# Moving large GpSimd operations to VectorE, and the first expert's input and weights in another order, ahead of a stream of 32 experts

## The chip, the cores and the metric

The kernel runs on one core of one Trainium2 chip. Inside the core five engines take their own instruction queues in parallel: TensorE (matrix products), VectorE, ScalarE and GpSimd (elementwise work), and SyncE, which here issues most of the DMA transfers. The metric is the device time of one execution in microseconds.

## The reference

One layer of a hybrid backbone is computed for 128 context rows and 256 latent rows of width 1024. The first half mixes an mLSTM head group and a Fourier head group behind one input projection and closes with a layer norm; the second half routes each row to 4 of 32 experts. Cut to what matters here:

```python
u = x * (1.0 + scale1) + shift1
p = u @ w_in                                   # q, k, v, o gate, gates, Fourier columns
h_m = layer_norm_per_head(mlstm(p)) * o_gate
f_m = fourier_mix(p[..., F_OFF:])              # Re of a 2-D DFT
mix = concatenate([h_m, f_m]) @ w_out
x = layer_norm(DEEPNORM_ALPHA * x + gate1 * mix, ln1_w, ln1_b)
u2 = x * (1.0 + scale2) + shift2
top_val, top_idx = lax.top_k(u2 @ router_w + router_b, TOP_K)
gates = softmax(top_val)
# for each expert e, on the rows that chose it:
h = xblk @ w_gu[e] + b_gu[e]
act = x_glu * sigmoid(SWIGLU_ALPHA * x_glu) * (x_lin + 1.0)
y += gate * (act @ w_down[e] + b_down[e])
x = layer_norm(DEEPNORM_ALPHA * x + gate2 * y, ln2_w, ln2_b)
```

All numbers are fp32, and the expert weights alone are 32 times 12 MB.

## The kernel before

The order is written out by hand: each engine runs its instructions in the order of the code, and waits there for whatever they need. So an instruction that waits holds up everything behind it on its engine.

**Phase 1, to about 180 us.** Modulation, input projection (`proj_T`, `proj_N`), mLSTM heads and Fourier groups. `proj_N(3, …)` computes the output gate (matmuls at L422); between its quarters it calls functions handed to it, in three gaps. Those that matter: `fourier_A` and `fourier_B` (VectorE L625 and L626, ScalarE L621 and L612), `head_norm` (VectorE L591), `mod_rest` (six small VectorE operations L668 to L673 on 64 partitions and less, which finish the modulation rows, and a DMA from ScalarE's queue, L674) and `wo_split`. The last cuts the output weights, eight pieces of 128x1024, into an upper part (ScalarE, L247) and the remainder (GpSimd, L249), since products of fp32 numbers are here summed from such parts. Pieces 0 to 3 belong to the first half of the output columns, 4 to 7 to the second. Then `ev_o` writes the gate: ScalarE's sigmoid (L491) and VectorE's product `og` (L492). TensorE transposes `og` (`heads_T`, L597), and L119, L120, L599 and L600 split the result.

**Phase 2, to about 241 us.** `out_mm` is the output projection (L853), `out_half` adds it to the residual (VectorE L860, L862, L864), `fold_1` and `fold_2` prepare the router's weights (VectorE L893 to L900, TensorE L904), `turn` transposes rows (TensorE L912, behind the L862 of the same rows), `router` gives the logits (L918), `top4` finds the four experts of each row (VectorE L923 to L946, for three groups of 128 rows: group 0 is the context, 1 and 2 the latent rows), and `places` counts (TensorE L950, behind L940 of `top4`). `out_norm(0)` normalises the context rows (ScalarE L883) and maps them to the expert's input with four GpSimd operations of 128x512 (L886, L887). `places_0` (VectorE L976, L977) and `gather_0` (TensorE L985) collect the rows of the first expert. How these follow each other is a string of steps (L1017): `m` is a part of the matmuls of rows 2, `h` of their `out_half`, `a` and `b` are single operations of the second and third `top4`, `A` and `B` their rest; letter and number are `P` places, `O` places_0, `T` turn, `R` router, `N` out_norm, `g` gather_0.

**Phase 3.** `experts` ends the order of the first stretch: the biases are split (L119, L120), and `modulate` maps the gathered rows to the first expert's input `XT0`, tiles 0 to 3 on ScalarE (L796), 4 to 7 on VectorE (L794), with an addition of 128x512 after each four (L797). Then 32 experts follow, each `gate_up` (L1163), activation, `down` (L1222), and spreading (L1107, L1241). Their weights are streamed by SyncE into a ring of tiles (`slot`, `fill`; the DMA issue is L755): a piece is issued when TensorE has finished with the piece whose tile it takes. The first expert's down projection is different (`load_dn`): piece 0 comes in two halves into the ring, piece 1 goes to tiles of its own (L781, L782).

## Time and profile before

| | |
|---|---|
| median of three runs | 1246.8 us (1244.35 to 1248.54) |
| profiled execution | 1248.78 us |
| its span, first to last instruction | 1247.1 us |
| mean granted clock of TensorE | 0.964 of full speed |
| TensorE busy | 1167.6 us (94%) |
| VectorE, ScalarE, GpSimd busy | 446.4, 229.0, 69.3 us |
| moved by DMA | 452.71 MB, mean 363 GB/s |

The span is read in three stretches: up to 180 us, where the work is varied; 180 to 244 us, where all engines work on the way to the first expert; and the experts, in which TensorE and the DMA engines are busy nearly all the time. A row of a timeline gives start, length, engine, line and tiles, and in brackets how long the engine stood idle before it and what ended that.

### The profile page before, as it was taken

To read this page: it belongs to the slowest core of one execution; us is meant where nothing else is said; L and a number is where in the kernel's file an instruction comes from. 1 tells how busy PE (TensorE), PEld (TensorE's weight loads), DVE (VectorE), ACT (ScalarE), POOL (GpSimd) and SP (SyncE) were. 2 spreads that over 40 slices of the span, in tenths; PEclk is the share of its full clock that TensorE was granted. 3 is DMA by queue.
4 is the path that set the end of the run, shared out by engine and by line. 5 is a ranking of instruction groups with operands and counts; after the bars stand their busy time and mean duration, and the time that the engine had idled before them with its cause. 6 is when DMAs were issued, how large, how long until landed. Compare 5 with 4: busy or idle time off the path is not lost.

```text
span 1247.1 us, 16409 instructions
## 1 busy us (share of the span) xinstructions
PE 1167.6 (94%) x6628; PEld 556.8 (45%) x6628; DVE 446.4 (36%) x944; ACT 229.0 (18%) x418; POOL 69.3 (6%) x79
## 2 busy tenths in 40 slices
PE   7999989799999999999999999999999999993874
PEld 4876768535335433434343353334435345331321
DVE  4444684623112431414323142332234124130415
ACT  2333341311211110201111121011111111111112
POOL 2001042200000000000000000000000000000301
PEclk9999989899899999999999999999999999996988
DMA  9977546499999999999999999999999899999993
GB/s 324 391 277 263 216 174 255 156 389 406 404 416 417 416 417 417 416 407 414 415 362 409 414 363 358 419 416 362 363 417 398 301 391 403 406 418 403 401 410 118
DMA packets 96978, 452.71 MB, mean 363 GB/s; under 512 B 8308, under 2 KB 18760, under 8 KB 62084
## 3 DMA queue, kind: packets, MB, share of 16 engines
q1 hardware_dynamic: 95088, 450.04, 91.0%
q10 hardware_dynamic: 1268, 1.31, 0.3%
q8 instruction: 54, 0.88, 0.3%
q0 software_dynamic: 544, 0.29, 0.1%
q14 instruction: 24, 0.20, 0.0%
HBM read 448.91 MB, written 2.70 MB: 362 GB/s over the span
## 4 chain that ended last, share of the span: by engine, by line
PE 84%; DMA 7%; DVE 5%; ACT 2%; issue 1%; SPq 1%; ACTq 0%; DVEq 0%
PE b L1163 38%; PE b L1222 19%; PE b L1241 4%; PE p L422 3%; DMA w<-in_w_gate_up_dram 3%; PE b L1107 3%; PE b L1171 2%; PE pm L853 2%; DMA w<-in_ln_w_dram 2%; PE b L1196 2%; DMA w<-in_w_ada_dram 1%; PE k L353 1%; ACT y L1228 1%; PE a L220 1%; DVE y L1230 1%
## 5 line engine op out<-in xcount | busy, mean ns | idle before, releaser
L1163 PE MATMUL b<-w,XT 128*64 128x512 f32 (+1 forms) x2560 | 496.2, 604 | 30.5 <-ACT w L1310 19.7
L1163 PEld LDWEIGHTS b<-w,XT 128*64 128x64 f32 (+1 forms) x2560 | 143.6, 129 | 332.2 <-issue 294.4
L1222 PE MATMUL b<-w,aT 128*64 128x512 f32 (+1 forms) x1596 | 248.3, 515 | 3.3 <-DMA w<-in_w_down_dram 3.2
L1182 DVE TENSOR_SCALAR g<-b 128x512 f32<-128x512 f32 (+1 forms) x40 | 24.5, 612 | 373.7 <-PE b L1171 293.9
L1222 PEld LDWEIGHTS b<-w,aT 128*64 128x64 f32 (+1 forms) x1596 | 81.6, 128 | 156.7 <-issue 141.9
L1230 DVE SCALAR_TENSOR_TENSOR y<-b,gc,y 64x512 fp32r<-64x512 f32 (+1 forms) x88 | 57.4, 652 | 217.6 <-ACT y L1228 217.3
L1228 ACT ACTIVATE y<-b,gc 64x512 fp32r<-64x512 f32 (+2 forms) x100 | 58.7, 587 | 292.1 <-PE b L1222 254.6
L1183 ACT ACTIVATE b<-g 128x512 f32<-128x512 f32 (+1 forms) x40 | 21.5, 538 | 353.6 <-DVE g L1182 353.4
L1246 DVE TENSOR_TENSOR yacc<-yacc,b 128x512 f32<-128x512 f32 x90 | 55.0, 680 | 0.0
L1107 PE MATMUL b<-O,tH 128*128 128x256 f32 x192 | 47.7, 289 | 4.5 <-DVE y L1230 4.5
L1241 PE MATMUL b<-y,OT 128*128 128x512 f32 x192 | 49.9, 405 | 0.0
L1317 POOL TENSOR_TENSOR XT<-tL,tH 128x384 f32<-128x384 f32 x2 | 2.0, 1006 | 841.5 <-PE b L1163 841.5
L1107 PE MATMUL b<-O,tL 128*128 128x256 f32 x192 | 46.5, 283 | 0.0
L1241 PEld LDWEIGHTS b<-y,OT 128*128 128x128 f32 x192 | 35.7, 193 | 13.9 <-issue 5.9
L1107 PEld LDWEIGHTS b<-O,tH 128*128 128x128 f32 x192 | 36.7, 191 | 10.2 <-DVE y L1230 5.3
L120 DVE TENSOR_TENSOR lw<-w,hw 128x1024 fp32r<-128x1024 f32 x20 | 24.4, 1222 | 34.9 <-ACT hw L119 34.7
L1107 PEld LDWEIGHTS b<-O,tL 128*128 128x128 f32 x192 | 36.7, 191 | 0.0
L1171 PEld LDWEIGHTS b<-bgu,pick 128*128 128x128 f32 x224 | 28.0, 189 | 18.7 <-issue 18.7
L1197 ACT ACTIVATE aT<-b 128x512 f32<-128x512 f32 (+1 forms) x40 | 21.3, 534 | 76.2 <-PE b L1196 70.9
L853 PE MATMUL pm<-w,mH 128*128 128x512 f32 x96 | 33.0, 426 | 0.0
L1171 PE MATMUL b<-bgu,pick 128*128 128x256 f32 x224 | 32.8, 292 | 0.0
L422 PE MATMUL p<-hw,uH 128*128 128x512 f32 x72 | 29.7, 412 | 1.7 <-ACT kq L412 1.7
(380 smaller groups left out, 1086.5 us busy)
## 6 DMA issues: line engine op xcount, KB each, us to landing
w<-in_w_gate_up_dram SPq DMA_DIRECT2D x113, 2048.0 KB, 13.4
w<-in_w_down_dram SPq DMA_DIRECT2D x52, 2048.0 KB, 15.5
w<-in_w_gate_up_dram SPq DMA_DIRECT2D x30, 1024.0 KB, 13.5
w<-in_w_down_dram SPq DMA_DIRECT2D x22, 1024.0 KB, 16.6
w<-in_w_ada_dram SPq DMA_DIRECT2D x8, 2048.0 KB, 7.6
w<-in_w_ada_dram SPq DMA_DIRECT2D x8, 1024.0 KB, 8.9
w<-in_w_in_dram SPq DMA_DIRECT2D x4, 2048.0 KB
w<-in_w_out_dram SPq DMA_DIRECT2D x2, 2048.0 KB, 8.8
```

The costliest lines, as they stand in the source:

```text
L422: PE.matmul(p[b], x, y, start=(k == 0 and t == 0), stop=(k == 7 and t == 2))
L853: PE.matmul(pm, x, y, start=(n == 0 and t == (part == 0) and part != 1), stop=(n == 7 and t == 2 and part != 0))
L1107: PE.matmul((pl if b else pc)[:, jj], t[b][:, (2 * i + jj) * 128:(2 * i + jj + 1) * 128], O[:, b], start=(b < 2 and q == 0), stop=(b != 1 ...
L1163: PE.matmul(p[g_][m * h:m * h + m], XT[:, k, o:o + m], rhs, start=(n_ == 0), stop=False, skip_group_check=True)
L1171: PE.matmul(p[g_][:, 256 * h:256 * h + 256], pick[2][:, h], bgu[:, q, 256 * g_:256 * g_ + 256], start=False, stop=(q == 1), skip_group_che ...
L1182: DVE.tensor_scalar(g, pg_, LIMIT, None, op0=OP.min)
L1196: PE.transpose(p[:, cc], s["act"][i][:, cc * 128:(cc + 1) * 128], ident)
L1222: PE.matmul(q[m * h:m * h + m, :f], aT[:, k, o:o + m], w[:, h * f:(h + 1) * f], start=(k == 0), stop=(k == 7))
L1228: ACT.activation(hi if plain else hi.bitcast(FR), dst, AF.Copy, scale=g)
L1230: DVE.scalar_tensor_tensor(y[1][o:o + m, h * f:(h + 1) * f].bitcast(FR), dst, g, hi, op0=OP.mult, op1=OP.subtract)
L1241: PE.matmul(p, OT[:, b * 128:(b + 1) * 128], y[q][:, hf * 512:(hf + 1) * 512].bitcast(FR), start=(u != 0 and q == 0), stop=(q == 1))
L1246: DVE.tensor_add(a, a, p)
```

## The change

There are four parts. The remainders of `wo_split` (L249) go from GpSimd to VectorE: those of pieces 2 and 3 into the second gap of `proj_N(3)`, piece 0 into the third, piece 1 behind `heads_T`, 4 to 7 where they stood in the code; in the second gap `mod_rest` now comes first. The context map goes from GpSimd to VectorE as two steps of the string, `X` behind `O0` and `Y` behind `g00`, and `g10` now stands between `P1` and `P2`. The first expert's input is mapped in the order in which TensorE uses its tiles, ahead of the bias split, with additions of 128x256. And of the first expert's down projection piece 1 is issued ahead of piece 0.

```diff
-            POOL.tensor_sub(l, w, h.bitcast(FT))
+            DVE.tensor_sub(l, w, h.bitcast(FT))
...
             wo_split(i, 0)
-            wo_split(i, 1)
-        proj_N(3, ev_o, lambda: (mod_loads(), fourier_B(0), fourier_A(2), head_norm(1), head_out(3), wo_split(2, 0), wo_split(2, 1), wo_split(3, 0), wo_split(3, 1)),
-               lambda: (fourier_B(1), fourier_A(3), mod_rest()),
-               lambda: (fourier_B(2), head_norm(2), head_norm(3), fourier_B(3)))
+        proj_N(3, ev_o, lambda: (mod_loads(), fourier_B(0), fourier_A(2), head_norm(1), head_out(3), wo_split(2, 0), wo_split(3, 0)),
+               lambda: (mod_rest(), fourier_B(1), fourier_A(3), wo_split(2, 1), wo_split(3, 1)),
+               lambda: (fourier_B(2), head_norm(2), head_norm(3), fourier_B(3), wo_split(0, 1)))
...
         heads_T()
+        wo_split(1, 1)
...
-        for i in range(2):
+        for i in (1, 0) if j == ORDER[0] else (0, 1):
...
-            for hs in halves:
-                POOL.tensor_mul(tX[b][:, hs], nc_[:, hs], bc["A", 1][:, hs])
-                POOL.tensor_add(tX[b][:, hs], tX[b][:, hs], bc["D", 1][:, hs])
+            context.append(nc_)
+
+        context = []
+
+        def context_map(hf):
+            hs = halves[hf]
+            DVE.tensor_mul(tX[0][:, hs], context[0][:, hs], bc["A", 1][:, hs])
+            DVE.tensor_add(tX[0][:, hs], tX[0][:, hs], bc["D", 1][:, hs])
...
-        for step in "P0 m m T1 m O0 R1 m g00 N1 h h T2 g01 a h a h a N2 a a a a R2 P1 b b b b b b b O1 P2 g11 A g10 O2 B C S g20 g21 E".split():
+        for step in "P0 m m T1 m O0 X R1 m g00 Y N1 h h T2 g01 a h a h a N2 a a a a R2 P1 b b b O1 b b b b g10 P2 A g11 O2 B C S g20 g21 E".split():
...
+        XT0 = mo.tile([128, 2, 8, 128], FT, name="XT", bufs=1)[:, 0]
+
+        for i, j in ((0, 2), (0, 3), (1, 4), (1, 5), (2, 2), (0, 0), (0, 1), (1, 6), (1, 7), (2, 0), (2, 4), (2, 6)):
+            p, a = xt[j // 4][:, j % 4], [aff[:, q, j:j + 1] for q in range(2)]
+            if i == 0:
+                ACT.activation(XT0[:, j], p, AF.Identity, bias=a[0], scale=a[1])
+            elif i == 1:
+                DVE.tensor_scalar(XT0[:, j], p, a[1], a[0], op0=OP.mult, op1=OP.add)
+            else:
+                DVE.tensor_add(XT0[:, j:j + 2], XT0[:, j:j + 2], xc[j // 4][:, j % 4:j % 4 + 2])
...
-        XT0 = mo.tile([128, 2, 8, 128], FT, name="XT", bufs=1)[:, 0]
-        for i in range(2):
-            modulate(XT0[:, 4 * i:4 * i + 4], 4 * i, xt[i], xc[i], i)
```

What moves on the engines is seen at three places. The first is VectorE in the second gap of `proj_N(3)`, before; `sm` are the modulation rows, `W` is what `fourier_B` writes, `lw` a part of a projection weight:

```order
L120 TENSOR_TENSOR lw<-w,hw 128x1024
L625 TENSOR_TENSOR W_1320<-a,y_1314 128x129
L626 TENSOR_TENSOR W_1320<-a,y_1314 128x127
L625 TENSOR_TENSOR W_1320<-a,y_1314 128x65
L626 TENSOR_TENSOR W_1320<-a,y_1314 128x63
L668 TENSOR_TENSOR sm<-sm 64x128
L669 SCALAR_TENSOR_TENSOR sm<-sm 64x64
L670 TENSOR_TENSOR sm<-sm 64x32
L671 COPY sm<-sm 64x32
L672 COPY sm<-sm 32x32
L673 TENSOR_TENSOR sm<-sm 32x32
L625 TENSOR_TENSOR W_1362<-a,y_1356 128x129
```

And the changed kernel there, where `w` at L249 is the remainder of an output weight:

```order
L120 TENSOR_TENSOR lw<-w,hw 128x1024
L668 TENSOR_TENSOR sm<-sm 64x128
L669 SCALAR_TENSOR_TENSOR sm<-sm 64x64
L670 TENSOR_TENSOR sm<-sm 64x32
L671 COPY sm<-sm 64x32
L672 COPY sm<-sm 32x32
L673 TENSOR_TENSOR sm<-sm 32x32
L625 TENSOR_TENSOR W_1323<-a,y_1317 128x129
L626 TENSOR_TENSOR W_1323<-a,y_1317 128x127
L625 TENSOR_TENSOR W_1323<-a,y_1317 128x65
L626 TENSOR_TENSOR W_1323<-a,y_1317 128x63
L249 TENSOR_TENSOR w<-w 128x1024 x2
```

The six operations of `mod_rest` have moved ahead of a Fourier group, and two remainders stand behind that group.

The second place is VectorE between the transposed gate (`mL`) and the residual (`pm`, `tX`), before:

```order
L600 SCALAR_TENSOR_TENSOR mL<-p_1426,cT_179,mH 128x384
L860 TENSOR_TENSOR pm<-pm,g1c 128x512
L862 SCALAR_TENSOR_TENSOR tX_69<-tX_69,pm 128x512
L864 BN_STATS s_1474<-tX_69 128x6
L860 TENSOR_TENSOR pm<-pm,g_1502 128x512
```

And in the changed kernel:

```order
L600 SCALAR_TENSOR_TENSOR mL<-p_1425,cT_179,mH 128x384
L249 TENSOR_TENSOR w<-w 128x1024 x5
L860 TENSOR_TENSOR pm<-pm,g1c 128x512
L862 SCALAR_TENSOR_TENSOR tX_69<-tX_69,pm 128x512
L864 BN_STATS s_1474<-tX_69 128x6
L860 TENSOR_TENSOR pm<-pm,g_1502 128x512
```

Five remainders, of pieces 1 and 4 to 7, now stand ahead of the first L860.

The third place is TensorE between the last `router` and the end of the gathers, before; `pp` are the counts, `xt` and `pm` the gathered rows, `lg` the logits:

```order
L985 MATMUL pm<-O_1490,tX_69 128x128 x4
L918 MATMUL lg<-rwA,uq 128x32 x4
L950 MATMUL pp<-sel,cst 128x32
L951 MATMUL pp<-sel,cst 128x64
L950 MATMUL pp<-sel,cst 128x32
L951 MATMUL pp<-sel,cst 128x32
L985 MATMUL xt<-O_1490,tX_70 128x128 x8
```

And in the changed kernel, in which the lines of `places` are L955 and L956, of `gather_0` L990 and of `router` L923:

```order
L990 MATMUL pm<-O_1490,tX_69 128x128 x4
L923 MATMUL lg<-rwA,uq 128x32 x4
L955 MATMUL pp<-sel,cst 128x32
L956 MATMUL pp<-sel,cst 128x64
L990 MATMUL xt<-O_1490,tX_70 128x128 x4
L955 MATMUL pp<-sel,cst 128x32
L956 MATMUL pp<-sel,cst 128x32
L990 MATMUL xt<-O_1490,tX_70 128x128 x4
L990 MATMUL xt<-O_1490,tX_71 128x128 x8
```

Half of the gather of rows 1 has moved in between the second and the third counting.

## Rows read from the trace of the kernel before

**Rows 1.** TensorE's timeline: start, length, line, tiles, [idle time before, releaser].
```profile
178.17 0.48 PE L597 MATMUL n<-cst,og 128*128 128x128 f32 x1 [5.75 <-DVE og L492]
...
221.24 0.56 PE L950 MATMUL pp<-sel,cst 128*128 128x32 f32 x2 [2.89 <-DVE sel L940]
...
228.44 1.05 PE L985 MATMUL pm<-O,tX 128*128 128x128 f32 x8
230.21 0.63 PE L912 MATMUL pu<-cst,tX 128*128 128x128 f32 x4 [0.72 <-DVE tX L862]
...
234.92 0.58 PE L950 MATMUL pp<-sel,cst 128*128 128x32 f32 x2 [1.72 <-DVE code L976]
...
235.74 5.09 PE L985 MATMUL xt<-O,tX 128*128 128x128 f32 x32
```

**Rows 2.** TensorE's waits, 244 to 1117 us: releaser, total, times, longest.
```profile
PE b L1163 <- issue: 3.1, 1, 3.1
```

**Rows 3.** Windows: engines' busy time, then granted clock, DMA share, GB/s.
```profile
221.00:225.00 4.00, 3.76 (x12) 3.13 (x13) 3.33 (x11) 0.00 (x0) 0.00 (x0) 0.57 0.99 418
235.00:248.00 13.00, 9.86 (x50) 7.20 (x52) 7.91 (x38) 4.86 (x8) 6.41 (x10) 0.76 0.14 40
332.00:348.00 16.00, 16.00 (x28) 5.02 (x30) 0.00 (x0) 2.39 (x4) 0.00 (x0) 0.51 1.01 418
```

**Rows 4.** SyncE's timeline: the first down-projection pieces.
```profile
246.87 3.05 SPq L755 DMA_DIRECT2D w<-in_w_down_dram  x2
```

**Rows 5.** GpSimd's timeline, 163 to 217 us.
```profile
163.18 9.51 POOL L249 TENSOR_TENSOR w<-w 128x1024 fp32r<-128x1024 f32 x4 [36.41 <-DVE lw L120]
...
183.41 9.64 POOL L249 TENSOR_TENSOR w<-w 128x1024 fp32r<-128x1024 f32 x4 [6.40 <-ACT w L247]
215.43 1.29 POOL L886 TENSOR_TENSOR tX<-g1c,prep 128x512 f32<-128x512 f32 x1 [22.38 <-ACT g1c L883]
```

**Rows 6.** VectorE's timeline, 160 to 200 us.
```profile
161.91 1.19 DVE L120 TENSOR_TENSOR lw<-w,hw 128x1024 fp32r<-128x1024 f32 x1
...
163.68 2.05 DVE L668 TENSOR_TENSOR sm<-sm 64x128 f32<-64x128 f32 x1
...
172.76 0.17 DVE L672 COPY sm<-sm 32x32 f32<-32x32 f32 x1
...
174.99 1.62 DVE L591 TENSOR_SCALAR og<-nm,mv 128x128 f32<-128x128 f32 x6
...
177.42 1.88 DVE L492 TENSOR_TENSOR og<-og,p 128x512 f32<-128x512 f32 x3 [0.15 <-ACT p L491]
...
182.68 0.61 DVE L600 SCALAR_TENSOR_TENSOR mL<-p,cT,mH 128x384 fp32r<-128x384 f32 x1
187.92 0.70 DVE L860 TENSOR_TENSOR pm<-pm,g1c 128x512 f32<-128x512 f32 x1 [4.63 <-PE pm L853]
...
193.41 0.70 DVE L860 TENSOR_TENSOR pm<-pm,g 128x512 f32<-128x512 f32 x1 [3.28 <-PE pm L853]
...
199.32 0.59 DVE L900 TENSOR_REDUCE prep<-prep 128x32 f32<-128x256 f32 x1
```

**Rows 7.** VectorE's timeline: first and last row of two `top4`.
```profile
215.49 0.25 DVE L923 SCALAR_TENSOR_TENSOR tiny<-csb,m,lg 128x32 f32<-128x32 f32 x1 [3.49 <-PE lg L918]
...
221.00 0.19 DVE L940 TENSOR_TENSOR sel<-sel,O 128x32 f32<-128x32 f32 x1
...
232.64 0.25 DVE L923 SCALAR_TENSOR_TENSOR tiny<-csb,m,lg 128x32 f32<-128x32 f32 x1 [0.16 <-PE lg L918]
...
234.57 0.19 DVE L940 TENSOR_TENSOR sel<-sel,O 128x32 f32<-128x32 f32 x1
```

**Rows 8.** ScalarE's timeline: upper parts of splits 4 to 7.
```profile
182.26 3.91 ACT L247 ACTIVATE w<-w 128x1024 fp32r<-128x1024 f32 x4
```

**Rows 9.** All engines' timeline ahead of the first expert matmul.
```profile
243.99 1.36 DVE L794 TENSOR_SCALAR XT<-xt,aff 128x128 f32<-128x128 f32 x4
...
244.17 2.67 PE L1163 MATMUL b<-w,XT 128*64 128x512 f32 x8 [3.14 <-issue]
```

More of the change, by code (lines that the diff above doesn't have):

```diff
@@ L1013, in tile_layer @@
         steps = dict(m=lambda: (next(m2_, 0), next(m2_, 0)), h=lambda: next(h2, 0), a=lambda: next(t1, 0), b=lambda: next(t2, 0),
-                     A=lambda: weave(t1), B=lambda: weave(t2), S=sort_1, C=lambda: DVE.tensor_copy(cnts, pp[:32, 3]), E=experts)
+                     A=lambda: weave(t1), B=lambda: weave(t2), S=sort_1, X=lambda: context_map(0), Y=lambda: context_map(1), C=lambda: DVE.tensor_copy(cnts, pp[:32, 3]), E=experts)
         next(m2_)
-        for step in "P0 m m T1 m O0 R1 m g00 N1 h h T2 g01 a h a h a N2 a a a a R2 P1 b b b b b b b O1 P2 g11 A g10 O2 B C S g20 g21 E".split():
+        for step in "P0 m m T1 m O0 X R1 m g00 Y N1 h h T2 g01 a h a h a N2 a a a a R2 P1 b b b O1 b b b b g10 P2 A g11 O2 B C S g20 g21 E".split():
             if step in steps:
```

## The prediction

> **What bounds the kernel now.** I read TensorE's rows first, since every later stage hangs on that engine. Up to 244 us it has four waits that matter, and each names VectorE: 5.75 us at L597 for `og`, 2.89 and 1.72 us at two of the countings (L950), 0.72 us at L912 [rows 1]. From 244 to 1117 us the view of its waits has three rows, none of which names a DMA; the one of interest is the 3.1 us ahead of the first expert matmul [rows 2]. Then I asked the windows what the weight stream does in between: from 235 to 248 us the DMA engines are 14% busy [rows 3], and the first pieces of the first down projection are issued at 246.87 us, after TensorE has freed a slot [rows 4]. So the ring is full and waits for TensorE when the experts start. A TensorE that starts earlier frees its slots earlier by as much, and the stream, whose start is those slots, moves with it. I therefore carry what is gained ahead of 244 us to the end in full; what the 1.7 us between span (1247.1) and profiled execution (1248.78) hold does not change.
>
> Why VectorE is late is read from GpSimd's and VectorE's rows side by side. While GpSimd subtracts at L249 from 163.18 to 172.69 us [rows 5], the 64x128 add at L668 takes 2.05 us; L672, which starts 0.07 us after GpSimd has ended, takes 0.17 [rows 6]. The first `top4` runs while GpSimd maps the context tile (from 215.43 us, four operations of about 1.3 us [rows 5]): from its first row to the end of its L940 it takes 5.70 us, and the third `top4`, same operations, takes 2.12 [rows 7]. But the L860 that starts at 187.92 us beside GpSimd's second group (183.41 to 193.05) takes 0.70, and the one at 193.41, after it, 0.70 too [rows 5, 6]: one of its inputs lies in PSUM.
>
> **Stage 1, to the router's L904.** `mod_rest` (L668 to L673) loses its neighbour: 9.46 us now (163.68 to 173.14); six operations, each between L672's 0.17 and 0.3, are 1.0 to 1.8, taken 1.4 [rows 6]. It now starts right behind the L120 that ends at 163.10, so ends at 164.5. The DMA issue and the Fourier activation behind it on ScalarE bring the next L625 group to about 165.8 (0.65 for the group). The splits cost VectorE what the L120 of the same 128x1024 shape costs: 1.2 each [rows 6]. So: group 166.4, splits 2 and 3 168.8, group 169.5, six L591 (1.62) 171.1, group 171.7, split 0 172.95. TensorE's projection ends at 172.42 (178.17 less its 5.75 of idle [rows 1]), ScalarE's sigmoid of one tile I take at the 0.6 of an `og` operation [rows 6]: `og` starts at 173.0 and L597 at 173.65, not 178.17. That is 4.5 us.
>
> Not all of it stays, because VectorE now is what is late. From the first `og` to the end of the last L600 is 5.87 us (177.42 to 183.29 [rows 6]), so 178.9; split 1 to about 180.2; only then may ScalarE write the upper parts of splits 4 to 7 into the freed slot (0.98 each [rows 8]), and the four remainders follow on VectorE, 180.2 + 1.0 + 4.9 = 186.1, ahead of the first L860. Behind ScalarE's wait stand three more upper parts and a table load, which nobody needs before TensorE's next L912; the weight pieces that wait on SP's queue for these tiles now come free at 186 instead of 193.05, GpSimd's end [rows 5]. That L860 was at 187.92, then 2.2 us for three operations; from the second L860 (193.41) to the end of the last L900 (199.91) it is 6.5 [rows 6]. With VectorE unbroken: 186.1 + 2.2 + 6.5 = 194.8. The L904 behind it comes **5.1 us** earlier. If TensorE's granted clock is low there too, I estimate 3.7 us: one spell near half clock, as in 221 to 225 us (0.57 [rows 3]), costs some 1.4.
>
> The Trainium skill (SBUF — State Buffer, Who interferes with whom) says that a VectorE instruction with two SBUF inputs contends with a GpSimd instruction that reads SBUF; the trace agrees (2.05 against 0.17 us), and it agrees in that the L860, with an input in PSUM, is not slowed. By that rule the second GpSimd group did VectorE no harm, and moving splits 4 to 7 only adds 4.9 us to VectorE's queue; by the sum above they are still better there, because four on GpSimd take 9.64 us and would end near 190, when TensorE now wants them by 187.
>
> **Stage 2, to the last gather.** The first `top4` falls from 5.70 to about 2.1, so its `sel` is there before TensorE asks: the 2.9 wait goes. The clock was 0.57 in 221 to 225 us [rows 3]; behind no wait it should stay, some 1.6 us back. The context map is now 4 x 0.7 = 2.8 us on VectorE, in two halves, of which the second stands ahead of the L860/L862 that L912 waits for: that wait stays at about 0.6. Four gather matmuls now stand between the second and the third counting (L950): eight records of 0.13 [rows 1], so about 0.9 of the 1.7 wait is filled and 0.8 left. Waits: 2.9 + 1.7 + 0.7 = 5.3 become 1.4, so 3.9; with the clock 5.5. The last 32 gather records took 5.09, 0.159 each, against 0.131 (1.05 for 8) some us before, at full clock [rows 1]; if the clock holds there as well, up to 1.3 more. **5.5 to 6.8, taken 6.1.**
>
> **Stage 3, the first expert.** Now ScalarE splits the biases (L119) and scales four tiles before VectorE can add and release the first expert matmul, at 244.17 after 3.14 idle; the four tiles that VectorE scales (0.34 each) come last [rows 9]. In the new order ScalarE scales two tiles ahead of all else, VectorE two behind its cast of the counts, and one 128x256 add releases TensorE: 241.03 + 0.2 (a small row such as L672) + 0.7 + 0.42 (between half and all of L860's 0.70 for 128x512 [rows 6]; the half and a start) = 242.4. The wait becomes 1.4, **1.7 us** gained. Whether the clock then falls as before is open: 0 to 1.5, taken 0.5. The bias split now stands behind the map, ahead of what the sorting (L1273 on) needs; the first 16 matmuls cover it. If that cover were gone, it would cost its 0.69.
>
> **The piece issued ahead.** 2 MB go out before the two halves that wait for TensorE, into DMA engines that are 14% busy [rows 3, 4]. No TensorE wait up to 1117 us is for a DMA [rows 2], so I take 0. A gain is excluded as long as that holds; the worst is that 2 MB delay a piece of the first expert by 5 us, which the ring, full at 235, hides.
>
> **Sum.** 5.1 + 6.1 + 1.7 + 0.5 = 13.4. Against the profiled execution 1248.78 - 13.4 = 1235.4; against the median, 1246.8 - 13.4 = **1233.4**. Lower ends 3.7 + 5.5 + 1.4 = 10.6, upper 5.1 + 6.8 + 1.7 + 1.5 = 15.1: 1231.7 to 1236.2. The three runs of before spread by 2 us about their median, so 1230 to 1238.
>
> **Rivals.**
> *VectorE's queue eats stage 1.* The hand-over between ScalarE and VectorE at splits 4 to 7 may not pipeline: with each upper part waiting for the remainder before it, it is 4 x (0.98 + 1.22) = 8.8 instead of 5.9. L860 then starts at 189.0 and L904 gains 2.2. For it: one more engine crossing in a queue that is now the late one. Against: the slots are four different ones. Sum 10.5, less a spell of low clock, 1.4: **1237.7**.
> *The stream does not follow.* If pieces land too late for the earlier TensorE, the half of the gain that the DMA engines cannot make up is lost: 6.7, **1240.1**. For it: after 250 us they are nearly always busy. Against: no DMA wait up to 1117 us [rows 2], and their idle 13 us ahead of the experts, which move along.
> *GpSimd is not the cause (slower).* If L668 to L673 and the first `top4` are slow of themselves, the splits just lengthen VectorE: three of 1.2 ahead of `og` make L597 3.7 later, split 1 and 4 to 7 (6.1) put L860 at 193.05 instead of 187.92, and L904 at 201.75, 1.8 later. The map's 2.8 go ahead of L912, less 0.9 filled: 1.9 later. Stage 3 gives 1.7 back. That is +2.0; both new waits are long enough for a spell of low clock, 1.6 each: +5.2, **1252.0**. It decides from the point at which `mod_rest` beside no GpSimd work takes over 7 us. Against it stand L672 and the third `top4`.
> *The clock stays low elsewhere.* From 332 to 348 us it was 0.51 with no wait that the trace shows [rows 3]; one spell like it costs 8 us: **1241.4**, faster still.
>
> **How the numbers follow.** Chances: the sum 0.66; VectorE's queue 0.12; the stream 0.09; clock 0.04; nothing of it arrives (a wait behind the ones I see takes all) 0.04; GpSimd not the cause 0.05. Range: 1230 to 1238 holds the first two, about 0.78 with their own tails; I take it to 1239.5 for the near side of the stream. The three runs can tell about 0.3% (3.7 us) from no change: faster 0.91, same 0.04, slower 0.05.
>
> **What would show it.** Right: L668 at 0.2 to 0.3 us; L597's wait near 1.2; first L860 near 186; no wait at the first counting; wait ahead of the first expert 1.4; TensorE's waits from there to 1117 less 14 without a DMA. Wrong: `mod_rest` still above 3 us; VectorE late by more than 2 us at L904; or DMA rows among the expert waits.

## The result and the profile after

| | before | after |
|---|---|---|
| median | 1245.9 us (4 runs, 1244.35 to 1248.54) | 1233.42 us (4 runs, 1232.08 to 1233.77) |
| ratio | | 0.9896, 95% interval 0.9876 to 0.9915 |
| profiled execution, its span | 1248.78, 1247.1 us | 1233.77, 1232.0 us |
| mean granted clock | 0.964 | 0.972 |

The kernel is 12.5 us faster by the medians. A second series gave 1233.73 us (5 runs, ratio 0.9904, 0.9888 to 0.992). The first part of the page of after, busy time by engine, shows what has moved: GpSimd falls from 69.3 to 46.2 us, and VectorE, which took the work over, does not rise (446.4 before).

```profile
PE 1159.1 (94%) x6628; PEld 550.2 (45%) x6628; DVE 446.0 (36%) x958; ACT 229.3 (19%) x418; POOL 46.2 (4%) x67
```

VectorE's total stays where it was because the 23 us taken over from GpSimd are done in half the time there, and because rows that stood still beside GpSimd now run at their own length. VectorE's timeline of after, 160 to 209 us (start, length, engine, line, operation, idle before it):

```profile
160.06 0.28 DVE L668 TENSOR_TENSOR sm<-sm 64x128 f32<-64x128 f32 x1
...
160.73 0.17 DVE L671 COPY sm<-sm 64x32 f32<-64x32 f32 x1
...
161.13 0.18 DVE L673 TENSOR_TENSOR sm<-sm 32x32 f32<-32x32 f32 x1
...
169.36 1.88 DVE L492 TENSOR_TENSOR og<-og,p 128x512 f32<-128x512 f32 x3
...
177.53 4.63 DVE L249 TENSOR_TENSOR w<-w 128x1024 fp32r<-128x1024 f32 x4 [1.19 <-issue]
182.08 0.69 DVE L860 TENSOR_TENSOR pm<-pm,g1c 128x512 f32<-128x512 f32 x1
...
206.27 0.25 DVE L928 SCALAR_TENSOR_TENSOR tiny<-csb,m,lg 128x32 f32<-128x32 f32 x1 [3.51 <-PE lg L923]
...
208.20 0.19 DVE L945 TENSOR_TENSOR sel<-sel,O 128x32 f32<-128x32 f32 x1
```

In before, the first of the two copies of `mod_rest` reads (VectorE's timeline of before):

```profile
170.30 2.43 DVE L671 COPY sm<-sm 64x32 f32<-64x32 f32 x1
```

L668 takes 0.28 us where it took 2.05 [rows 6], and that copy 0.17 where it took 2.43; the first `top4` takes 2.12 us (206.27 to 208.39) where it took 5.70 [rows 7]; the four remainders of pieces 4 to 7 take 4.63 us where GpSimd took 9.64 [rows 5].

TensorE's timeline of after, its waits on the way to the experts and behind the first of them (L597, L909, L917, L990, L1175 and L1308 are L597, L904, L912, L985, L1163 and L1296 of before):

```profile
170.09 0.33 PE L597 MATMUL n<-cst,og 128*128 128x128 f32 x1 [0.64 <-DVE og L492]
...
190.74 0.49 PE L909 MATMUL pu<-prep,cst 128*128 128x128 f32 x2 [0.57 <-DVE prep L905]
...
219.99 1.16 PE L990 MATMUL xt<-O,tX 128*128 128x128 f32 x8 [0.74 <-DVE tiny L934]
...
221.62 2.92 PE L990 MATMUL xt<-O,tX 128*128 128x128 f32 x24
225.98 3.65 PE L1175 MATMUL b<-w,XT 128*64 128x512 f32 x16 [1.24 <-DVE XT L1047]
...
240.87 0.37 PE L1308 MATMUL b<-itm,cst 32*1 32x64 f32 x2 [3.57 <-DVE itm L1290]
...
241.19 6.72 PE L1175 MATMUL b<-w,XT 128*64 128x512 f32 x24
```

The waits of 5.75, 2.89, 1.72 and 3.14 us [rows 1, 9] are 0.64, none, 0.74 and 1.24. But there is a wait that the kernel before did not have: 3.57 us at L1308, the matmul that hands out the sorted list in the midst of the first expert, and the 24 matmuls behind it take 6.72 us. In before the same place reads as follows (TensorE's timeline of before): no wait, and 5.37 us for the 24.

```profile
257.12 0.27 PE L1296 MATMUL b<-itm,cst 32*1 32x64 f32 x2
...
257.34 5.37 PE L1163 MATMUL b<-w,XT 128*64 128x512 f32 x24
```

**Where the new wait comes from.** GpSimd's and then VectorE's timeline of after, 225 to 241 us:

```profile
230.35 2.51 POOL L1057 TENSOR_SCALAR cT<-cT 4x512 f32<-4x512 f32 x1 [3.80 <-DMA cT<-in_ln_b_dram]
...
234.57 1.03 POOL L1080 CAST tL<-y 128x1024 fp32r<-128x1024 f32 x1
```

```profile
235.64 1.23 DVE L1078 TENSOR_TENSOR y<-tX,tH 128x1024 fp32r<-128x1024 f32 x1 [4.14 <-POOL tL L1080]
...
240.54 0.27 DVE L1290 SCALAR_TENSOR_TENSOR itm<-cst,cl,itm 32x64 f32<-32x64 f32 x1
```

It is read backwards. TensorE waits for `itm`; that stands in VectorE's queue behind three halvings (L1078), each of which needs the cast that GpSimd makes of the one before (L1080); and those casts stand in GpSimd's queue behind L1057, which scales two small rows of norm parameters and waits 3.80 us for their DMA. In before that row reads (GpSimd's timeline of before):

```profile
243.56 1.51 POOL L1042 TENSOR_SCALAR cT<-cT 4x512 f32<-4x512 f32 x1 [1.37 <-DMA cT<-in_ln_b_dram]
```

So the rows came 2.43 us later and the scaling itself took 1.00 us more, beside VectorE's L1078 that starts at 230.28; GpSimd's queue is 3.4 us later by the two. Not all of that reaches TensorE, since the first cast in before stood idle for its input: the experiments below take 2.5 of the 3.57 us away with the delay of the rows, and 1.1 us stay. What delayed the rows is the fourth part of the change: the 2 MB piece goes out at 215.10 now, behind other weights, and when the small rows are issued (225.47 and 226.00 us) the DMA engines are full, at a share of 1.03 (the windows of after):

```profile
225.00:227.00 2.00, 1.02 (x6) 0.45 (x8) 2.00 (x7) 2.00 (x4) 1.07 (x2) 1.00 1.03 414
```

**The account.** One thing has to be taken off first. At the end of `proj_N(3)`, ahead of everything that the change touches, the profiled execution of after is already 2.96 us ahead. The windows from 30 to 40 us, of before and then of after, show why (length, busy time of PE, PEld, DVE, ACT and POOL with counts, granted clock, DMA share, GB/s): the clock was 0.66 there in the one execution and 1.00 in the other. Executions of the other kernels, which change nothing there either, show 0.83 and 1.00, so this belongs to an execution, not to a kernel.

```profile
30.00:40.00 10.00, 8.96 (x43) 6.07 (x44) 2.33 (x7) 0.86 (x4) 0.00 (x0) 0.66 1.08 368
```

```profile
30.00:40.00 10.00, 9.14 (x60) 7.64 (x60) 3.83 (x9) 3.24 (x6) 0.00 (x0) 1.00 1.08 367
```

| stretch, by starts of TensorE's rows | before | after | gained | forecast |
|---|---|---|---|---|
| up to L904, less the 2.96 | 199.97 | 190.74 | 6.27 | 5.1 |
| L904 to the end of the gathers (L963) | 40.79 | 33.73 | 7.06 | 6.1 |
| L963 to the first expert matmul | 3.41 | 1.51 | 1.90 | 1.7 |
| first 16 expert matmuls, to L1273 | 5.28 | 3.58 | 1.70 | 0.5 |
| L1273 to the hand-out of the list (L1296) | 7.67 | 11.31 | -3.64 | 0 |
| the next 24 matmuls and what follows, to L1196 | 9.53 | 11.08 | -1.55 | 0 |
| from there to the end of the span | 980.45 | 980.05 | 0.40 | 0 |
| sum | | | 12.14 | 13.4 |

The lines are those of before, in us. The sum of 12.1 us agrees with the 12.5 us by the medians. From L1196 on next to nothing is lost or gained in these two executions: what TensorE has then, it has at the end.

### The profile page after: what moved, and what is told of

The parts are those of the page before. It is cut to its first block, busy times and chain, and to the rows that moved or that the text cites. A ratio compares the mean times of both kernels' runs of the same rounds, so it can differ in the third digit from the quotient of the medians.

```text
span 1232.0 us, 16404 instructions
## 1 busy us (share of the span) xinstructions
PE 1159.1 (94%) x6628; PEld 550.2 (45%) x6628; DVE 446.0 (36%) x958; ACT 229.3 (19%) x418; POOL 46.2 (4%) x67
## 4 chain that ended last, share of the span: by engine, by line
PE 73%; DMA 7%; DVE 4%; ACT 1%; issue 1%; POOL 0%; ACTq 0%; DVEq 0%; POOLq 0%
PE b L1175 38%; PE b L1234 19%; DMA w<-in_w_gate_up_dram 4%; PE b L1253 4%; PE b L1119 3%; PE b L1183 3%; DMA w<-in_ln_w_dram 2%; PE b L1208 2%; PE pm L853 1%; ACT y L1240 1%; DVE y L1242 1%; PE b L1251 1%; PE b L1144 1%; PE b L1142 1%; PE b L1179 0%
## 5 line engine op out<-in xcount | busy, mean ns | idle before, releaser
L1175 PE MATMUL b<-w,XT 128*64 128x512 f32 (+1 forms) x2560 | 496.0, 604 | 28.5 <-ACT w L1322 19.7
L1175 PEld LDWEIGHTS b<-w,XT 128*64 128x64 f32 (+1 forms) x2560 | 143.2, 129 | 330.7 <-issue 290.9
```

The lines of the kernel that those rows point to most:

```text
L1175: PE.matmul(p[g_][m * h:m * h + m], XT[:, k, o:o + m], rhs, start=(n_ == 0), stop=False, skip_group_check=True)
```

## The experiments

Changes "to after" are made in the kernel after, changes "to before" in the kernel before. A kernel's line numbers can be one off against those above.

### Each part alone, on the kernel before

These four ask whether the gains come from where the prediction put them. All share 35 runs of before, median 1246.93 us. The gains named here are by the ratio.

**Part 1 alone: the remainders.**

```diff
-            POOL.tensor_sub(l, w, h.bitcast(FT))
+            DVE.tensor_sub(l, w, h.bitcast(FT))
```

with the new places of `wo_split` and `mod_rest` from the diff of the change.

> The kernel before with the first part of the change alone: the remainders of the output weights on VectorE at the new places, mod_rest first in its gap. By the prediction's first term L904 comes 5.1 us earlier: 1240.8. By the trace of the changed kernel, in which the stretch from the end of the Fourier group to L904 shrank by 6.3 us: 1239.6. If the first part only prepares the others: within 2 us of before, 1245.9.

Measured: 1242.73 us (12 runs), ratio 0.9964 (0.9944 to 0.9984), 4.5 us less. L904 comes 6.3 us earlier than in before, the 1.1 us that this execution had ahead of the change left out; that is what the whole change has there. The view of TensorE's waits from 140 to 260 us, of this kernel, shows the wait at L597 down from 5.75 to 0.65 us and the others as they were:

```profile
PE pp L950 <- DVE sel L940: 3.0, 1, 3.0
...
PE n L597 <- DVE og L492: 0.7, 1, 0.7
```

Not all of the 6.3 us arrives: at L1196 3.8 of them are left, in part because in this execution the gathers take 5.45 us (5.09 in before) and the first 16 expert matmuls 6.52 (5.35).

**Part 2 alone: the context map.**

```diff
-            for hs in halves:
-                POOL.tensor_mul(tX[b][:, hs], nc_[:, hs], bc["A", 1][:, hs])
-                POOL.tensor_add(tX[b][:, hs], tX[b][:, hs], bc["D", 1][:, hs])
+            context.append(nc_)
```

with `context_map`, the steps `X` and `Y`, and the new string.

> The kernel before with the second part alone: the context map on VectorE as two steps, and the new order of the steps. By the prediction's second term 6.1 us earlier at the first expert: 1239.8; by the trace of the changed kernel 7.1 us: 1238.8. Rival: the four VectorE operations just take the place of the wait; then the wait ahead of L912 grows by more than 1 us and the time is above 1243.

Measured: 1241.74 us (12 runs), ratio 0.9961 (0.9945 to 0.9976), 4.9 us less. Here it is the other way round: 5.8 us at L597 remain, and no wait at the first counting is left in the view. The map and the new order of the steps were not run apart.

**Part 3 alone: the first unit's map.**

```diff
-        XT0 = mo.tile([128, 2, 8, 128], FT, name="XT", bufs=1)[:, 0]
-        for i in range(2):
-            modulate(XT0[:, 4 * i:4 * i + 4], 4 * i, xt[i], xc[i], i)
```

with the new loop ahead of the bias split.

> The kernel before with the third part alone: the first expert's input mapped in the order of use ahead of the bias split. By the prediction 1.7 us and 0.5 for the clock: 1243.7; by the trace of the changed kernel 1.9 us and 1.7 for a clock that stays up: 1242.3. If the wait of the sorting (L1308 of the changed kernel, none before) comes from this part, as the bias split now stands ahead of the sorting on VectorE: a wait of 2 us and more there, and no gain: 1246.

Measured: 1244.88 us (12 runs), ratio 0.999 (0.9973 to 1.0007): a gain of 1.2 us that the interval does not tell from none. TensorE's timeline shows the gain and, already here, a first piece of the wait at the hand-out:

```profile
239.74 3.65 PE L1171 MATMUL b<-w,XT 128*64 128x512 f32 x16 [1.26 <-DVE XT L1043]
...
252.13 0.27 PE L1304 MATMUL b<-itm,cst 32*1 32x64 f32 x2 [1.07 <-DVE itm L1286]
...
252.36 5.37 PE L1171 MATMUL b<-w,XT 128*64 128x512 f32 x24
```

**Part 4 alone: the piece ahead.**

```diff
-        for i in range(2):
+        for i in (1, 0) if j == ORDER[0] else (0, 1):
```

> The kernel before with the fourth part alone: piece 1 of the first down projection issued ahead of piece 0. By the prediction 0: 1245.9. In the kernel before the 2 MB would be issued at about 229 us and land by 236 to 240, just ahead of GpSimd's question for its rows at 242, so no collision. If the collision needs no earlier TensorE: the wait of L1042 for its rows grows beyond 3 us, and a wait of about 3 us appears at the sorting: 1249.

Measured: 1250.56 us (12 runs), ratio 1.0027 (1.001 to 1.0043), **3.4 us slower**. The prediction's 0 is refuted. ScalarE's and TensorE's timeline of this kernel:

```profile
243.22 0.63 ACT L119 ACTIVATE bgu<-aT 128x512 fp32r<-128x512 f32 x1 [9.38 <-DMA aT<-in_b_gate_up_dram]
```

```profile
246.12 5.57 PE L1163 MATMUL b<-w,XT 128*64 128x512 f32 x16 [5.27 <-issue]
```

The piece goes out at 228.88 us, the bias rows at 236.74, and they land late, 5.1 us after their issue where they took 2.2 in before (medians of the four rows): ScalarE's bias split, which in this order stands ahead of the map of the first unit, waits for a DMA, and the first expert matmul stands idle for 5.27 instead of 3.14 us. That is 2.1 of the 3.4 us; where the rest lies is not settled.

**The sum of the parts.** Parts 1 to 3 alone give 4.5 + 4.9 + 1.2 = 10.6 us, each with some 2 us of uncertainty, and the whole 12.5: within that they add up. Part 4 costs 3.4 us alone. In the whole, part 3 puts the bias split behind the map; and in the trace of part 3 alone GpSimd issues the bias rows 11.1 us ahead of L963, where it is 3.6 in before. In after it is 8.8 us, and nothing waits for these rows. So that cost is off TensorE's way, and what is left of the early piece is the later wait at L1308. This is read from the traces; parts 3 and 4 were not run together without the others.

### The wait at the hand-out of the list

**The old order of pieces in the kernel after.** To after:

```diff
-        for i in (1, 0) if j == ORDER[0] else (0, 1):
+        for i in range(2):
```

> The changed kernel with the two pieces of the first down projection in the old order, all else as changed. Theory: the 2 MB issued ahead fill the DMA engines in 224 to 230 us, so the layer-norm rows that GpSimd waits for (L1057) take 3.8 us after it asks instead of 1.4; GpSimd's casts, VectorE's halving and the sorting queue up behind, and TensorE waits 3.57 us at L1308 and then runs 1.35 us longer at low clock. Then here the wait of L1057 falls to about 1.4, that at L1308 under 0.7, and the time is about 4 us under the changed kernel's 1233.4, so 1229. Rival 1: the sorting chain is simply uncovered because TensorE came early; then the wait at L1308 stays above 3 us and the time at 1233. Rival 2: the early piece is worth something of its own; then some weight wait appears in the first expert and the time is above 1233.

Measured: 1234.2 us (6 runs, 1230.23 to 1235.99), ratio 0.9903 (0.9873 to 0.9933). GpSimd's and TensorE's timeline:

```profile
231.43 1.65 POOL L1057 TENSOR_SCALAR cT<-cT 4x512 f32<-4x512 f32 x1 [1.36 <-DMA cT<-in_ln_b_dram]
```

```profile
241.91 0.27 PE L1308 MATMUL b<-itm,cst 32*1 32x64 f32 x2 [1.08 <-DVE itm L1290]
...
242.13 7.07 PE L1175 MATMUL b<-w,XT 128*64 128x512 f32 x24
```

The trace confirms the cause: without the early piece the DMA engines are nearly idle when the rows are issued (a share of 0.04), GpSimd waits 1.36 us for them, as in before, and TensorE's wait is 2.5 us shorter.

```profile
229.00:231.00 2.00, 1.49 (x8) 0.62 (x10) 2.00 (x7) 2.00 (x3) 1.07 (x2) 1.00 0.04 8
```

```profile
234.25 1.22 DVE L1078 TENSOR_TENSOR y<-tX,tH 128x1024 fp32r<-128x1024 f32 x1
```

(The first row is from the windows of this kernel, the second from VectorE's timeline.) The other executions agree: with the early piece in the changed kernel GpSimd waits from 2.05 to 4.04 us in four of them, without it from 1.36 to 1.55 in seven. The time does not show it. The clock was low behind the wait of 1.08 us as well (24 matmuls in 7.07 us), and in this execution it was low in the gathers too (24 in 3.84 us instead of 2.92).

**The scaling later.** To after, with its GpSimd work moved behind the sorting:

```diff
-        POOL.tensor_scalar(rows1, rows1, ALPHA, None, op0=OP.mult)
...
-        inside = {0: [lambda: [halve(b) for b in range(NB)]], 2: [sort_2], 5: [sort_3]} ...
+        inside = {0: [lambda: [halve(b) for b in range(NB)]], 2: [sort_2, lambda: POOL.tensor_scalar(rows1, rows1, ALPHA, None, op0=OP.mult)], 5: [sort_3]} ...
```

> The changed kernel with the new piece order kept, and GpSimd's scaling of the layer-norm rows (the instruction that waits for their DMA) moved behind its three casts and the sorting. Theory (GpSimd's queue holds the chain up): the first cast starts as soon as VectorE has written its input, near 231.5 us instead of 234.6; the wait at L1308 falls from 3.57 to about 0.3 and the clock stays up: 1228.8. Rival 1 (the chain itself is too long): the wait stays above 2.5 us and the time at about 1233.

Measured: 1233.71 us (6 runs, 1231.2 to 1238.74), ratio 0.9904 (0.9872 to 0.9937).

**Both.** To after, the two edits above together.

> The changed kernel with the old piece order and the scaling moved behind the casts. Theory: either alone clears the queue, so both together give what one gives, 1228.8, within 1 us of the run with only the scaling moved. If the early piece had a worth of its own, this run is slower than that one by more than 1 us; if the two costs were separate, it is faster by more than 1 us.

Measured: 1232.82 us (6 runs, 1230.7 to 1236.29), ratio 0.9895 (0.9866 to 0.9925). In both kernels the wait at the hand-out is 0.9 us, not the 0.3 or less expected, and the 24 matmuls behind it take 7.07 us. GpSimd's queue is not what holds the chain there: in its timeline of the kernel with the scaling later, the first cast waits for VectorE.

```profile
236.13 1.04 POOL L1079 CAST tL<-y 128x1024 fp32r<-128x1024 f32 x1 [3.48 <-DVE y L1077]
```

The three halvings and three casts, 2.36 us from one to the next, by themselves end later than TensorE comes. So it was not enough to free GpSimd's queue; the chain itself had to be taken out of the way. Both times miss the 1228.8 expected; in both traces the gathers ran at low clock as well (24 in 5.47 us).

**The sorting ahead of two halvings.** To after:

```diff
-        inside = {0: [lambda: [halve(b) for b in range(NB)]], 2: [sort_2], 5: [sort_3]} ...
+        inside = {0: [lambda: halve(0)], 2: [sort_2, lambda: [halve(b) for b in range(1, NB)]], 5: [sort_3]} ...
```

> The changed kernel (new piece order kept) with two of the three halvings (ScalarE L1077, VectorE L1078, GpSimd L1080) moved behind the first sorting step, so that VectorE's part of the sorting waits for no GpSimd cast. Theory: the wait at L1308 has two parts, 1.1 us because the first expert now begins earlier than three halvings in a row can end (seen as 1.08 with the old piece order and as 1.07 in the run with the third part alone), and 2.5 us because GpSimd's casts stand behind rows that the early piece delays. Here both go: no wait at L1308, no spell of low clock behind it (1.5), 5 us in the trace and 3 to 5 in the median against the changed kernel run beside it: 1229 to 1230. Rival: what the wait hides is the next wait (weights, or the activation behind the first expert); then TensorE's wait moves to a later line and the time stays within 1.5 us.

Measured: 1232.39 us (4 runs, 1227.19 to 1234.82), ratio 0.9892 (0.9875 to 0.9909); the kernel after beside it, 1233.73. That is 1.3 us, less than the 3 to 5 us expected and inside the spread of the runs.

**The same with the old order of pieces.** To after, this edit and that of the old order together.

> The same with the pieces in the old order. Theory: with the sorting out of GpSimd's way the early piece neither costs nor gives anything: within 1.5 us of the run with the new order. If the early piece has a worth (the halves of piece 0 find freer DMA engines), this run is slower by more than 1.5 us; if it still collides somewhere, faster by more.

Measured: **1230.84 us** (4 runs, 1229.56 to 1231.75), ratio 0.9871 (0.9855 to 0.9887). TensorE's timeline of this last kernel:

```profile
239.99 0.27 PE L1308 MATMUL b<-itm,cst 32*1 32x64 f32 x2
...
240.22 5.37 PE L1175 MATMUL b<-w,XT 128*64 128x512 f32 x24
```

In both kernels the wait is gone, the clock stays up and the 24 matmuls take 5.37 us. The version with the old order of pieces is the fastest measured, 2.9 us below after in the same series by the medians; every one of its four runs is below the median of after, but one run of after (1230.98) lies among them. Whether the piece ahead still costs something once the sorting stands first (1232.39 against 1230.84) is not settled: the runs overlap.

**The kernel after once more,** without an edit.

> The changed kernel once more, beside the others. By its first times 1233.4. The two profiles so far differ by 3 us ahead of 158 us, where the change touches nothing: one more profile tells whether TensorE's clock at 30 to 40 us (0.66 in the kernel before, 1.00 in the changed one) belongs to the change (then 1.00 again) or to the single execution (then either).

Measured: 1233.73 us (5 runs, 1230.98 to 1237.29). The wait is there again, 1.53 us, with the rows 2.76 us late, and the 24 matmuls take 7.07 us (TensorE's and GpSimd's timeline):

```profile
240.37 0.27 PE L1308 MATMUL b<-itm,cst 32*1 32x64 f32 x2 [1.53 <-DVE itm L1290]
...
240.59 7.07 PE L1175 MATMUL b<-w,XT 128*64 128x512 f32 x24
```

```profile
230.85 1.51 POOL L1057 TENSOR_SCALAR cT<-cT 4x512 f32<-4x512 f32 x1 [2.76 <-DMA cT<-in_ln_b_dram]
```

So the wait belongs to the kernel, and its length varies: 3.57 and 1.53 us in two executions.

### GpSimd as the cause

**Pieces 4 to 7 back on GpSimd.** To after:

```diff
-            DVE.tensor_sub(l, w, h.bitcast(FT))
+            (DVE if i < 4 else POOL).tensor_sub(l, w, h.bitcast(FT))
```

> The changed kernel with the remainders of pieces 4 to 7 given back to GpSimd; pieces 0 to 3 stay on VectorE. Theory: GpSimd needs 9.6 us for them where VectorE needs 4.6, so TensorE's second half of the output projection is held until about 187 instead of 182.5; VectorE's first L860 comes earlier, near 178, but the second, and with it L909, about 3 us later: 1236.5 (+3). Rival, by the rule that VectorE's L860, with an input in PSUM, is not held up by GpSimd: VectorE's queue is freed of 4.6 us, L909 comes earlier, 1232 or less.

Measured: 1236.05 us (6 runs, 1234.89 to 1237.6), ratio 0.9925 (0.9896 to 0.9953); the three kernels of the section above, on the same chip, 1234.2, 1233.71 and 1232.82. The median is near the one expected, but its trace doesn't bear out the mechanism in full. GpSimd's, VectorE's and TensorE's timeline:

```profile
177.25 9.61 POOL L249 TENSOR_TENSOR w<-w 128x1024 fp32r<-128x1024 f32 x4 [7.97 <-ACT w L247]
```

```profile
177.59 0.70 DVE L860 TENSOR_TENSOR pm<-pm,g1c 128x512 f32<-128x512 f32 x1 [1.52 <-PE pm L853]
...
185.38 1.51 DVE L900 COPY aff<-csb 128x16 f32<-128x16 f32 x1
```

```profile
190.95 0.49 PE L909 MATMUL pu<-prep,cst 128*128 128x128 f32 x2 [1.54 <-DVE prep L905]
```

GpSimd takes 9.61 us for what VectorE does in 4.63. VectorE's L860, one input in PSUM, is not slowed beside it (0.70); a copy of 128x16 that takes 0.17 us in after stands until GpSimd ends and takes 1.51. TensorE's L909 comes 0.2 us later than in after (0.5 with what this execution was ahead before that), not 3. So this trace shows only a small loss, and the 2 to 3 us of the medians are inside the spread of these kernels.

**GpSimd only writes.** To before, zeros in place of the remainders of pieces 0 to 3:

```diff
+            if i < 4:
+                POOL.memset(l.bitcast(FT), 0.0)
+            else:
+                POOL.tensor_sub(l, w, h.bitcast(FT))
-            POOL.tensor_sub(l, w, h.bitcast(FT))
```

> The kernel before, in which GpSimd writes zeros to the remainders of pieces 0 to 3 in place of subtracting: same place, same output tile, no input read (the output projection then lacks these remainders). By the rule that VectorE with two SBUF inputs contends only with a GpSimd operation that reads SBUF: L668 to L673 take 1.1 us as in the changed kernel, og comes at about 173.4 and L597 4.5 us earlier; time 1242. Rival: any GpSimd operation on a large tile holds VectorE: L668 stays above 1 us as long as GpSimd is busy, and the time near 1246.

Measured: 1237.83 us (4 runs), ratio 0.9923 (0.9907 to 0.994). It did not make the meeting it was meant to make. The writes need nothing but a free tile and ran earlier than the subtractions, so GpSimd was idle beside `mod_rest`. GpSimd's and VectorE's timeline:

```profile
155.45 3.64 POOL L250 MEMSET w<- 128x1024 f32 x4 [29.89 <-ACT w L247]
```

```profile
157.82 1.03 DVE L580 TENSOR_TENSOR nm<-nm,den 128x384 f32<-128x384 f32 x2
...
162.47 0.27 DVE L671 TENSOR_TENSOR sm<-sm 64x128 f32<-64x128 f32 x1
```

It tells something all the same. With `mod_rest` at its old place and no subtraction moved to VectorE, the six operations take 1.25 us instead of 9.46, and L597 comes 5.9 us earlier, the 1.2 us that this execution was ahead before that left out. That is the cause alone, without the new order: GpSimd's subtraction held `mod_rest`. The median is 8.5 us below that of before, more than the 4 expected and more than part 1 gives; the traced execution, the slowest of the four (1242.58), shows 5.2 us at L1199, the L1196 of before, those 1.2 us left out, and where the rest comes from stays open. And the two operations of VectorE at L580, with both inputs in SBUF, which run wholly beside the writes, take 1.03 us; the same two take 1.03 in before, where GpSimd is idle there. The Trainium skill (SBUF — State Buffer, Who interferes with whom) says that VectorE with two SBUF inputs contends with a GpSimd instruction that reads SBUF and not with one that only writes it; these rows agree with both halves.

## Why the prediction was right, and where it was not

The time, 1233.42 us, is the one forecast, 1233.4, and the mechanism is the one forecast for the parts that carry the gain. That the two numbers agree to a tenth is luck: the gains were put some 4 us too low, a new wait that costs 5.2 us was not seen, and the median of before, 1246.8 in the prediction, is 1245.9 with the fourth run, so that 12.5 us were gained and not 13.4.

- **What bounds the kernel, right.** A TensorE that starts the experts earlier takes the weight stream with it. From L1196 to the end the two traces differ by 0.4 us over 980, and the view of TensorE's waits from 236 to 1103 us of after names no DMA:

```profile
PE b L1119 <- DVE y L1242: 4.5, 4, 1.4
PE b L1308 <- DVE itm L1290: 3.6, 1, 3.6
PE b L1208 <- DVE g L1198: 1.0, 1, 1.0
```

  The stream is close behind, though. In after once more the same view names DMA rows, 3.1 and 1.4 us, which the prediction gave as a sign that it is wrong; they come where TensorE's clock stays full (the last point of this list).

- **Stage 1, right, 1.2 us too low.** With the 2.96 us put back, the group at L625 starts at 165.4 (165.8 forecast), the first `og` product at 172.3 (173.0), the first L860 at 185.0 (186.1). The wait at L597 is 0.64 us, 1.2 forecast. The remainders of 4 to 7 pipeline: 4.63 us for the four, so the rival in which ScalarE and VectorE take turns (8.8 us) is out. The prediction's pair for GpSimd's harm, 2.05 against 0.17 us, compares two different operations; L668 itself takes 0.28.
- **Stage 2, right, 0.96 us too low.** No wait at the first counting; 0.71 at L917 (0.6 forecast) and 0.74 in place of the 1.72 (0.8 forecast). The rest is the clock: it was granted in full through the gathers (24 in 2.92 us, where before has 32 in 5.09 [rows 1]), the end of the range that I had not taken. That end was summed wrongly: 32 times the difference of 0.159 and 0.131 is 0.9 us and not 1.3, and the 32 now take 4.08 (1.16 and 2.92), 1.0 less. Nor is it the kernel's own: in after once more the 24 took 3.84. The windows of after, 172 to 238 and 240 to 244 us, show 1.00 and then 0.57:

```profile
172.00:238.00 66.00, 61.70 (x341) 46.37 (x339) 45.14 (x127) 24.55 (x45) 9.51 (x12) 1.00 0.82 302
240.00:244.00 4.00, 3.13 (x12) 1.25 (x14) 1.68 (x8) 0.00 (x0) 0.34 (x1) 0.57 0.00 0
```

- **Stage 3, right in the wait, 1.2 us too low in the clock.** The wait ahead of the first expert is 1.24 us (1.4 forecast). The 16 matmuls behind it take 3.65 us where they took 5.35; I had allowed up to 1.5 us for this and taken 0.5.
- **The piece issued ahead, wrong.** The step that failed is "No TensorE wait up to 1117 us is for a DMA, so I take 0". That view lists what TensorE waits for. It does not list for what the engines wait that TensorE waits for, and there stood a row of before that I had not read: 1.37 us of GpSimd for a DMA of 4 KB, which is 3.80 in after. Alone, the part costs 3.4 us by another such row: ScalarE's bias split, 2.1 us late.
- **"The first 16 matmuls cover it", wrong.** I held the bias split against the time of the 16 matmuls and left out that TensorE now does them 1.7 us faster, and that the sorting hangs on the halvings, not on the split. Counted from the first expert matmul, with the old order of pieces, TensorE asks for the list 1.6 us sooner than in before (11.32 us for 12.95, the wait left out), and the first halving starts 0.7 us later (4.7 us for 4.0); from there to `itm` the chain takes what it took. In before the list was ready about 1.3 us ahead of TensorE (`itm` ended at 255.78 us, TensorE came at 257.12), so 1.1 us of waiting come out, which is what the old order of pieces (1.08) and part 3 alone (1.07) show. Part 3 alone also shows that it is not the 13 us gained up to the end of the gathers that make TensorE wait there: it has none of them. VectorE's timeline of before:

```profile
248.18 1.22 DVE L1066 TENSOR_TENSOR y<-tX,tH 128x1024 fp32r<-128x1024 f32 x1
```

  This and the late rows are the 5.2 us: 3.64 of waiting, and 1.55 behind it, of which 1.35 are the 24 matmuls at low clock.
- **GpSimd not the cause (slower), out.** `mod_rest` takes 1.25 us without GpSimd beside it (160.06 to 161.31), far from the 7 us that this rival needed.
- **The clock elsewhere, mis-priced.** I gave 8 us to a spell such as that from 332 to 348 us [rows 3]. The profiled executions of after once more and of the kernel with the sorting ahead have none: the clock was 1.00 from 310 to 350 us, and the same work runs 15 to 18 us earlier there. (The profiled execution of after has it: 0.50 from 320 to 330.) Against before they gain only 3.2 and 3.6 us between L1196 and 380 us, because TensorE at full clock there runs into the weight stream and waits some 4 us; the DMA engines are full there, at a share of 1.00 to 1.03 from 310 to 350 us. No other trace has such a wait between 236 and 1117 us (TensorE's timeline of the kernel with the sorting ahead):

```profile
336.87 1.93 PE L1234 MATMUL b<-w,aT 128*32 128x256 f32 x32 [1.11 <-DMA w<-in_w_down_dram]
...
341.86 3.65 PE L1175 MATMUL b<-w,XT 128*64 128x512 f32 x16 [3.05 <-DMA w<-in_w_gate_up_dram]
```

## What to carry to other kernels

Before a large transfer is moved ahead of others, list what every engine waits for, not only the one that bounds: a 4 KB row behind a 2 MB piece made its reader wait 0.7 to 2.7 us longer here, and it stood at the head of a chain that ended at TensorE. When an engine is made faster, look past the wait that goes to the chains that used to end in time behind it, and ask what slack they had and what pace they have of their own (the list was ready 1.3 us ahead here); the fix here was to put the short chain (the sorting) ahead of the long one (the halvings), not to make either faster. And small operations of VectorE that take seven to fourteen times their length beside a GpSimd row are a sign that the row, and not their own work, should be moved.

## What the runs showed of the hardware that was not expected

- **Copies stop too.** The prediction spoke of operations with two SBUF inputs. In before the copy at L671 (64x32) took 2.43 us beside GpSimd and 0.17 alone, and in the kernel with pieces 4 to 7 on GpSimd the copy of 128x16 took 1.51 instead of 0.17. The Trainium skill (SBUF — State Buffer, Who interferes with whom) lists copies among the operations that can take both ports; these two rows agree.
- **Each small operation waited out one GpSimd instruction.** L668 to L671 took 2.05, 2.27, 2.30 and 2.43 us in before, beside GpSimd subtractions of 2.38 us (9.51 for four [rows 5]), whatever their own length (0.28 to 0.17 us in after). So the price of such a meeting was the number of small operations times the length of the large one.
- **It goes both ways.** GpSimd's L1057 took 2.51 us when VectorE's L1078 had started 0.07 us before it, and ended 1.4 us after L1078 did; in after once more it took 1.51 us.
- **Low clock does not follow from the length of a wait.** Behind 1.07 us at the hand-out (part 3 alone) the 24 matmuls took 5.37 us, behind 1.08 us (old order of pieces) 7.07, at 1.53 us 7.07 and at 3.57 us 6.72; without a wait 5.37. (From 241 to 244 us the granted clock was 0.54 in after once more and 1.00 with the sorting ahead.) Likewise the gathers took from 2.92 to 5.47 us for 24 in kernels that are alike up to there. What decides it stays open. It may be why kernels that differ by 1 to 2 us of waiting could not be told apart by their medians: single executions of one changed kernel lie up to 7.6 us apart, and of before up to 11.
